# Two more tile pairs in the feed-forward blocks of a hybrid layer: FFN 2's tiles 2 and 3, and a fifth pair in FFN 1's w2

## The chip, the cores and the metric

The kernel runs on one core of one Trainium2 chip. The metric is the device time of one execution in microseconds, the median of several runs. A core has five engines with instruction queues of their own: TensorE (PE; its weight loads are shown as PEld), VectorE (DVE), ScalarE (ACT), GpSimd (POOL) and SyncE (SP), which here issues nearly all DMA transfers. Each queue is worked off in order, and engines wait for each other through semaphores.

## The reference

One layer on 512 tokens with a model width of 1024, all in float32:

```
f = swiglu(rms_norm(x, g1), w1a, w3a, w2a)        # FFN 1, hidden width 2816
h = x + 0.5 * rms_norm(f, post1)
u = rms_norm(h, mix_pre)
q, k, v, x_rnn, x_gate = split(u @ w_in)
y_a = (rg_lru(causal_conv(x_rnn)) * gelu(x_gate)) @ w_lru_out
y_b = sliding_window_attention(q, k, v, sinks, bias) @ w_attn_out
g = sigmoid(u @ w_gate + b_gate)
h = h + rms_norm((g[0] * y_a + g[1] * y_b) @ w_o, mix_post)
f = swiglu(rms_norm(h, g2), w1b, w3b, w2b)        # FFN 2, the same shape
y = h + 0.5 * rms_norm(f, post2)

swiglu(x, w1, w3, w2) = (silu(x @ w1) * (x @ w3)) @ w2
```

## The kernel before

Every float32 operand is split into a rounded part ("hi", in the fp32r format) and a remainder ("lo"): ScalarE rounds, VectorE subtracts. A product is then three matmuls: hi x hi, lo x hi, hi x lo. Activations lie transposed in one big buffer, uT (hi and lo, 8 blocks of 128 features, 512 tokens). Everything else lives in a pool of 43 equal buffers of 4 KB per partition (`NSLOT`), which are taken when a tile is first written and come free after its last reader.

The hidden width of 2816 is 22 tiles of 128. A tile of w1 or w3 is worked in one of two ways.

- A plain *unit* (`unit`, `mm_feat`): 8 blocks x 3 matmuls with 512 columns, 24 matmuls.
- A *pair job* (`class Pairs`): two neighbouring tiles of one matrix are multiplied with x as a 2 x 2 block product after Strassen and Winograd, with 7 products in place of 8. A product (`mm_s`) is 12 matmuls with 256 columns, so a job is 84 matmuls. For x it needs the blocks b11, b21, b22 and the sums t1 to t4 (`sums`, `to_slots`, `to_uT`). For the weights it needs sums and differences of the four blocks, split into hi and lo. `prep(m, i)` makes these for job m in five steps (0: four sums; 1 to 3: one tile split each; 4: half a tile), and `run` calls those of the next job between the products of the current one. The product with t4 of a job is issued behind the second product of the following job.

`NC1 = 6` and `NC2 = 4` say how many tiles of FFN 1 and FFN 2 go as plain units; the others are pair jobs (16 and 18 of them).

The last product of an FFN, hidden x w2 (`w2_gemm`), has four token tiles by two halves of 512 columns, accumulated in all eight PSUM banks. `W2` gives its order: so many plain tiles, then groups of tile pairs (again 7 products for 8; here a pair is 42 matmuls of 512 columns, where two plain tiles are 48), then plain tiles, then the last `RF` tiles, which `tok_finish` works token tile by token tile, so that norm and transposes of one token tile run beside the next one's matmuls. FFN 1 has 6 plain tiles, one group of 4 pairs, 2 plain tiles and 6 last ones. FFN 2 has 2, two groups of 4 pairs, and 4 last ones. A plan inside `w2_gemm` with costs and due times orders the splits, sums and differences for VectorE and ScalarE.

For some pairs of w2 the weight parts t1 and t2, b22, t3 and t4 are made long before, in stages with free time, stored to device memory and loaded again when needed (`pre_pair`, `PRE`, `PRE_AT`): FFN 2's pairs 2, 4, 6, 8 and 14.

Work that is to run beside the matmuls is put off with `later(n, fn, rank)`: it is emitted at the n-th `point()` from there. Points lie after half a unit (12 matmuls) or after one product of a pair job; among work due at one point the lower rank goes first.

`post_norm` takes the mean square of a token tile from PSUM (ScalarE squares and sums two halves), gets the reciprocal root through a square root, a reciprocal and one Newton step on VectorE, and adds the residual. `norms` does this and then the next block's first norm. Before FFN 2 the code runs the output projection `wo` by `tok_gemm`, whose end works the first two tiles of w1b and w3b in half-units of 256 columns.

Of the kernel before, what the change touches and what calls it, by code (L numbers as in the profile page):

```python
# [12 lines left out]
AF = mybir.ActivationFunctionType  # L13
ALU = mybir.AluOpType

P = 128
SEQ = 512
D = 1024
# [8 lines left out]
EPS = 1e-6  # L27
# [24 lines left out]
def hybrid_layer(ctx: ExitStack, tc: tile.TileContext, a: dict, out: bass.AP):  # L52
# [126 lines left out]
    def later(n, fn, rank=1):  # L179
        uid[0] += 1  # L180
        due.append((now[0] + n, rank, uid[0], fn))
# [63 lines left out]
    def bcast(name):  # L245
# [2 lines left out]
        pool.dma_start(out=t, in_=bass.AP(tensor=src.tensor, offset=src.offset, ap=[[0, P], [1, D]]))  # L248
        return t

    def post_norm(acc, res, gpost, scale, dst, after=None):

        ss = small(2, "ss")
        fg = slot([P, D], name="fg")
        junk = slot([P, D], name="junk")
        cs = [slice(n * 512, (n + 1) * 512) for n in range(2)]
        for n, c in enumerate(cs):
            act.activation(junk[:, c], acc[n], AF.Square, accum_out=ss[:, n : n + 1])
        dve.tensor_tensor(out=fg[:, cs[0]], in0=acc[0], in1=gpost[:, cs[0]], op=ALU.mult)
        s1 = small(1, "s1")  # L260
        dve.tensor_tensor(out=s1, in0=ss[:, 0:1], in1=ss[:, 1:2], op=ALU.add)
        r = rstd_of(s1, scale, lambda: dve.tensor_tensor(out=fg[:, cs[1]], in0=acc[1], in1=gpost[:, cs[1]], op=ALU.mult))
        for n in range(2):
            c = slice(n * 512, (n + 1) * 512)
            dve.scalar_tensor_tensor(out=dst[:, c], in0=fg[:, c], scalar=r, in1=res[:, c], op0=ALU.mult, op1=ALU.add)
            if after:
                after(n, c)

    def norms(acc, t, res, gpost, scale, gpre, keep):

        hg = slot([P, D], name="hg")
        junk = slot([P, D], name="junk")
        ss = small(2, "ss")

        def half(n, c):
            act.activation(junk[:, c], res[:, c], AF.Square, accum_out=ss[:, n : n + 1])
            dve.tensor_tensor(out=hg[:, c], in0=res[:, c], in1=gpre[:, c], op=ALU.mult)

        post_norm(acc, res, gpost, scale, res, half)
        sp.dma_start(out=keep[t], in_=res)  # L280
        s1 = small(1, "s1")
        dve.tensor_tensor(out=s1, in0=ss[:, 0:1], in1=ss[:, 1:2], op=ALU.add)
        r = rstd_of(s1)
        dve.tensor_scalar(out=hg[:, :512], in0=hg[:, :512], scalar1=r, scalar2=None, op0=ALU.mult)
        act.activation(hg[:, 512:], hg[:, 512:], AF.Copy, scale=r)
        return hg
# [147 lines left out]
    def pre_pair(nm, f, at0, step):  # L434
        made = PRE_TILES.setdefault(nm, {})
        dram = [tc.dram_tile([P, D], F32, name=f"pre_{nm}{f}_{i}") for i in range(5)]
        made[f] = [dram[:2], *dram[2:]]
        r, t = [], {}

        def load():  # L440
            for n in range(2):
                r.append(slot([P, D], name="rawp"))
                src = a[nm][f * P : (f + 2) * P, n * 512 : n * 512 + 512]
                sp.dma_start(out=r[n].rearrange("p (b c) -> p b c", b=2), in_=src.rearrange("(b p) c -> p b c", p=P))

        def hi(name, src, w=QH):
            if w == D:
                t[name] = slot([P, D], F32R, name="ph"), slot([P, D], F32R, name="pl")
            else:
                x = slot([P, 2, QH], F32R, name="pb")  # L450
                t[name] = x[:, 0, :], x[:, 1, :], x
            t[name] = *t[name], src
            act.activation(t[name][0], src, AF.Copy)

        def lo(name):
            x = t[name]
            dve.tensor_tensor(out=x[1], in0=x[-1], in1=f32(x[0]), op=ALU.subtract)
# [12 lines left out]

        steps = [
            (load,),
            (),
            (lambda: hi("t12", t12_of(*r), D),),
            (lambda: lo("t12"), lambda: hi("b22", r[1][:, QH:])),
            (lambda: store(0, "t12"), lambda: lo("b22")),
            (sums34, lambda: store(1, "b22")),
            (lambda: lo("t3"), lambda: hi("t4", r[0][:, QH:])),
            (lambda: store(2, "t3"), lambda: lo("t4"), lambda: r.clear()),
            (lambda: store(3, "t4"),),  # L480
        ]
        for i, fns in enumerate(steps):
            later(at0 + i * step, lambda fns=fns: [fn() for fn in fns], 4)

    def pre_at(where):
        for nm, f, at_, step in PRE_AT.get(where, ()):
            pre_pair(nm, f, at_, step)

# [347 lines left out]
    QH = 4 * P  # L836
# [13 lines left out]
    class Pairs:  # L850
# [13 lines left out]
        def prep(self, m, i):  # L864
            if m >= len(self.jobs):
                return
            k = self.k0 + 2 * m
            if i == 0:
# [119 lines left out]
    def load_w(u, kp):  # L988
        nm, i = order[u]
        c = slice(kp * 2 * P, (kp + 1) * 2 * P)  # L990
        sp.dma_start(out=raw3[u][:, c], in_=a[nm][i * P : (i + 1) * P, c])


    warm = slot([P, 512], F32R, name="warm")
# [3 lines left out]
        pe.matmul(psw, warm[:, :P], warm, start=True, stop=True)  # L998

    load_x(0, act)  # L1000
    sp.dma_start(out=vec, in_=a["vec"])
    for kp in range(KT // 2):
        load_w(0, kp)
        if kp:
            load_x(2 * kp)
        load_w(1, kp)
        load_w(2, kp)
        load_x(2 * kp + 1)
    dma_to(NS + 2)
# [4 lines left out]
    hid, X1 = Hidden("w2a"), {}  # L1014
# [115 lines left out]
    def uview(hh, th):  # L1130

        return lambda e, k: uT[:, e, 4 * hh + k, th * 256 : th * 256 + 256]
# [1 line left out]
    def pair_view(p):  # L1134
        return lambda e, k: p[e][:, k, :]

    def sums(xf):

        t = [slot([P, 4, 256], name="T") for _ in range(4)]
        dve.tensor_tensor(out=t[0], in0=xf[0, 1], in1=xf[0, 0], op=ALU.subtract)  # L1140
        dve.tensor_tensor(out=t[2], in0=xf[1, 1], in1=xf[0, 1], op=ALU.subtract)
# [43 lines left out]
    def w2_ahead():  # L1185
# [301 lines left out]
    def emit_step(n):  # L1487
# [2 lines left out]
            bias_load(g + 1)  # L1490
        att_s(g, j)

    w_lru = get("lru", 0)
    point(True)
    bias_load(0)
# [44 lines left out]
    hid = Hidden("w2b")  # L1540
    X2, tn = {"b11": uview(0, 0), "b21": uview(1, 0), "b22": uview(1, 1)}, []
# [3 lines left out]
    later(2, lambda: xf.clear())  # L1545
    for i in range(3):
        later(2 + i, lambda i=i: X2.update({f"t{i + 1}": to_slots(tn[i])}))
    pairs_b = Pairs("w1b", "w3b", NC2, X2, hid)
    end = 2 * 2 * (NC2 - 2)
    for i, at_ in enumerate((end - 7, end - 4, end - 3, end - 2, end - 1)):  # L1550
        later(at_, lambda i=i: pairs_b.prep(0, i))
    later(end, lambda: pairs_b.prep(1, 0))
    swiglu_units("w1b", "w3b", 2, NC2, hid)
    point(True)
    X2["t4"] = to_uT(tn[3], 0, 1)
    tn.clear()
    pairs_b.run(w2_ahead)
    X2 = pairs_b = None
    w2_gemm("w2b", hid, "ffn2_post_g", 0.5, None, [], h2, None)


# [16 lines left out]
W2_LOAD = (14, 9, 8, 8)  # L1578
P0A, P0B = 6, 8
W2_LEAD = 2.5  # L1580
# [1 line left out]
W2_FLUSH = 2.5  # L1582

NC1 = 6
NC2 = 4


# [52 lines left out]
```

## Time and profile before

| | |
|---|---|
| median of 3 runs | 1120.51 us (1120.48 to 1120.9) |
| the profiled execution | 1120.09 us, span 1118.3 us |
| granted TensorE clock, mean | 0.999 |
| TensorE busy / its weight loads busy | 99% / 88% of the span |
| VectorE / ScalarE / GpSimd busy | 81% / 54% / 3% |
| instructions on TensorE | 6613 matmuls, 6613 weight loads |

The span runs from the first to the last instruction; some 1.8 us of the execution lie around it. Matmuls are pipelined, and their ends are modelled: one that is shown with 0.39 us may start 0.23 us after the one before, so the spacing of the starts is what a matmul costs. The stages follow each other so: FFN 1's w1 and w3 to 234 us, its w2 to about 350 us, the mixer's projections, recurrent branch and attention to about 724 us, `wo` to 799 us, FFN 2's w1 and w3 to 1002 us, its w2 to the end.

### The profile page before, as it was taken

The numbers are of one execution on the slowest core, as the hardware profiler recorded it, in microseconds if no ns is written. First come the engines' busy times: TensorE is split into PE (matmuls) and PEld (weight loads), VectorE is DVE, ScalarE is ACT, GpSimd is POOL, SyncE is SP. The second block draws the span as 40 slices with busy tenths as digits, with TensorE's granted clock in tenths as the row PEclk, the third lists the DMA queues.
The fourth block names the chain that finished last, engine by engine and source line by source line (L and its number), as shares of the span: only waits on it lengthen the run. The fifth ranks groups of instructions, "written<-read, shape, count | busy, mean of one in ns | idle before, by whom it ended". The sixth has DMA issues, their size and how long they took to land.

```text
span 1118.3 us, 17215 instructions
## 1 busy us (share of the span) xinstructions
PE 1109.7 (99%) x6613; PEld 987.7 (88%) x6613; DVE 907.3 (81%) x1609; ACT 607.8 (54%) x1072; POOL 34.7 (3%) x60
## 2 busy tenths in 40 slices
PE   9999999999999999999999999999999999999997
PEld 7889999988889887888888888888999999998886
DVE  5999888888887777886799877777868888887995
ACT  7555555564455368945655664355644555555352
POOL 0000000000000000001021111000000000000000
PEclk9999999999999999999999999999999999999999
DMA  9863332260554444536232335562333322357543
GB/s 343 148 165 102 114 96 94 77 225 1 173 203 159 162 156 149 182 117 225 76 95 76 95 95 218 199 241 79 133 121 104 114 90 101 95 205 268 178 177 113
DMA packets 50482, 161.12 MB, mean 144 GB/s; under 512 B 5536, under 2 KB 7072, under 8 KB 50400
## 3 DMA queue, kind: packets, MB, share of 16 engines
q1 hardware_dynamic: 47808, 151.33, 39.3%
q0 software_dynamic: 2448, 8.43, 4.0%
q8 instruction: 52, 0.85, 0.3%
q10 hardware_dynamic: 144, 0.26, 0.1%
q14 instruction: 30, 0.25, 0.1%
HBM read 136.42 MB, written 22.54 MB: 142 GB/s over the span
## 4 chain that ended last, share of the span: by engine, by line
PE 98%; ACT 1%; DMA 1%; DVE 0%; DVEq 0%; issue 0%
PE f L205 12%; PE f L207 12%; PE f L206 12%; PE c L845 10%; PE c L847 10%; PE c L846 10%; PE acc L223 5%; PE acc L224 5%; PE acc L225 5%; PE acc L719 3%; PE acc L721 3%; PE acc L720 3%; PE pt L1446 1%; PE s L1410 1%; DMA t<-pre_w2b 1%; PE tr L294 1%
## 5 line engine op out<-in xcount | busy, mean ns | idle before, releaser
L205 PE MATMUL f<-uT,whi 128*128 128x512 f32 (+1 forms) x536 | 196.7, 367 | 0.0
L207 PE MATMUL f<-uT,whi 128*128 128x512 f32 (+1 forms) x536 | 195.2, 364 | 0.0
L206 PE MATMUL f<-uT,wlo 128*128 128x512 f32 (+1 forms) x536 | 195.1, 364 | 0.0
L205 PEld LDWEIGHTS f<-uT,whi 128*128 128x128 f32 x536 | 101.2, 189 | 16.9 <-issue 1.4
L845 PE MATMUL c<-Xh,whi 128*128 128x256 f32 x408 | 115.6, 283 | 0.1
L847 PE MATMUL c<-uT,whi 128*128 128x256 f32 x408 | 115.5, 283 | 0.0
L846 PE MATMUL c<-Xh,wlo 128*128 128x256 f32 x408 | 115.5, 283 | 0.0
L846 PE MATMUL c<-uT,wlo 128*128 128x256 f32 x408 | 115.5, 283 | 0.0
L847 PE MATMUL c<-Xl,whi 128*128 128x256 f32 x408 | 115.5, 283 | 0.0
L845 PE MATMUL c<-uT,whi 128*128 128x256 f32 x408 | 115.5, 283 | 0.0
L207 PEld LDWEIGHTS f<-uT,whi 128*128 128x128 f32 x536 | 101.1, 189 | 16.2
L206 PEld LDWEIGHTS f<-uT,wlo 128*128 128x128 f32 x536 | 101.2, 189 | 15.6
L196 DVE TENSOR_TENSOR wlo<-S,whi 128x1024 fp32r<-128x1024 f32 x68 | 82.9, 1219 | 16.4 <-ACT whi L195 16.4
L845 PEld LDWEIGHTS c<-Xh,whi 128*128 128x128 f32 x408 | 78.3, 192 | 0.3 <-ACT ct L920 0.3
L846 PEld LDWEIGHTS c<-uT,wlo 128*128 128x128 f32 x408 | 78.3, 192 | 0.0
L845 PEld LDWEIGHTS c<-uT,whi 128*128 128x128 f32 x408 | 78.3, 192 | 0.0
L846 PEld LDWEIGHTS c<-Xh,wlo 128*128 128x128 f32 x408 | 78.3, 192 | 0.0
L847 PEld LDWEIGHTS c<-uT,whi 128*128 128x128 f32 x408 | 78.3, 192 | 0.0
L847 PEld LDWEIGHTS c<-Xl,whi 128*128 128x128 f32 x408 | 78.3, 192 | 0.0
L195 ACT ACTIVATE whi<-S 128x1024 fp32r<-128x1024 f32 x68 | 68.2, 1050 | 0.0
L223 PE MATMUL acc<-whi,hT 128*128 128x512 f32 x160 | 62.5, 390 | 0.0
L224 PE MATMUL acc<-wlo,hT 128*128 128x512 f32 x160 | 62.3, 389 | 0.0
(406 smaller groups left out, 2741.6 us busy)
## 6 DMA issues: line engine op xcount, KB each, us to landing
raw_w2a<-in_w2a_dram SPq DMA_DIRECT2D x22, 512.0 KB, 4.6
raw_w1b<-in_w1b_dram SPq DMA_DIRECT2D x22, 512.0 KB, 4.5
raw_w3b<-in_w3b_dram SPq DMA_DIRECT2D x22, 512.0 KB, 4.5
raw_w3a<-in_w3a_dram SPq DMA_DIRECT2D x21, 512.0 KB, 4.2
raw_w1a<-in_w1a_dram SPq DMA_DIRECT2D x20, 512.0 KB, 4.6
raw_w2b<-in_w2b_dram SPq DMA_DIRECT2D x17, 512.0 KB, 4.1
h<-h SPq DMA_DIRECT2D x16, 512.0 KB, 3.7
raw_wg<-in_wg_dram SPq DMA_DIRECT2D x16, 512.0 KB, 3.9
```

Of the source, the lines that this page charges most:

```text
L195: act.activation(hi, src, AF.Copy)
L196: dve.tensor_tensor(out=lo, in0=src, in1=f32(hi), op=ALU.subtract)
L205: pe.matmul(ps[:, c0:c1], wh[:, s], h_, start=k == 0, stop=False)
L206: pe.matmul(ps[:, c0:c1], wl[:, s], h_, start=False, stop=False)
L207: pe.matmul(ps[:, c0:c1], wh[:, s], l_, start=False, stop=k == KT - 1)
L223: pe.matmul(acc[n], x[:, 0, c], wh[:, s], start=first, stop=False, skip_group_check=True)
L224: pe.matmul(acc[n], x[:, 0, c], wl[:, s], start=False, stop=False, skip_group_check=True)
L225: pe.matmul(acc[n], x[:, 1, c], wh[:, s], start=False, stop=last, skip_group_check=True)
L719: pe.matmul(b, h[:, c], wh, start=start and n_ == 0, stop=False, skip_group_check=True)
L845: pe.matmul(ps, wh[:, s], xh, start=first, stop=False, skip_group_check=True)
L846: pe.matmul(ps, wl[:, s], xh, start=False, stop=False, skip_group_check=True)
L847: pe.matmul(ps, wh[:, s], xl, start=False, stop=k == 3, skip_group_check=True)
```

## The change

- FFN 2's tiles 2 and 3 are no longer plain units but a pair (`NC2 = 2`, 20 pair jobs). The first job's weights are loaded and prepared during the attention output projection (`FIRST_AT`, with a new step -1 of `prep` that only loads). The sums of x are made directly behind `wo`, with t1 split in between, and t3 and t4 are split inside the first job.
- FFN 1's w2 has one group of 5 pairs in place of 4 and no plain tiles behind it. The first of the five (tile 6) has its parts made during FFN 1's pair jobs 9 to 15 in finer steps (`PRE_JOB`), stored, and loaded in w2.
- FFN 2's stored pairs 2, 8 and 14 are made in the x_rnn stage from points 1, 6 and 11 on; pair 14 was made in the attention output stage, pairs 2 and 8 from points 2 and 8 on.
- The norms get a shorter chain: the first half's mean square is scaled as soon as it is there, ScalarE's square root takes it as bias, constant factors move into the scaling of the data, and the Newton step is one instruction shorter.
- At the start one of the first weight blocks is issued from ScalarE's queue instead of SyncE's.

The core of the diff:

```diff
+    def sum_half(ss, n, junk, src, c):
+        act.activation(junk[:, c], src, AF.Square, accum_out=ss[:, n : n + 1])
+    def first_half(ss):
+        v0 = small(1, "v0")
+        dve.tensor_scalar(out=v0, in0=ss[:, 0:1], scalar1=1.0 / D, scalar2=EPS, op0=ALU.mult, op1=ALU.add)
+        return v0
+    def root(ss, v0):
+        s = small(1, "s")
+        act.activation(s, ss[:, 1:2], AF.Sqrt, scale=1.0 / D, bias=v0)
+        return s
+    def factor(ss, v0, s):
+        v, r, e, r2 = (small(1, x) for x in ("v", "r", "e", "r2"))
+        dve.scalar_tensor_tensor(out=v, in0=ss[:, 1:2], scalar=1.0 / D, in1=v0, op0=ALU.mult, op1=ALU.add)
+        dve.reciprocal(r, s)
+        dve.scalar_tensor_tensor(out=e, in0=r, scalar=v, in1=r, op0=ALU.mult, op1=ALU.mult)
+        dve.scalar_tensor_tensor(out=r2, in0=e, scalar=-3.0, in1=r, op0=ALU.add, op1=ALU.mult)
+        return r2
...
     def post_norm(acc, res, gpost, scale, dst, after=None):
...
+        for n in range(2):
+            sum_half(ss, n, junk, acc[n], cs[n])
+        scaled(0)
+        v0 = first_half(ss)
+        s = root(ss, v0)
+        scaled(1)
+        r = factor(ss, v0, s)
...
+        if nm == "w2a":
+            s = []
+            steps = [
+                (load,), (), (),
+                (lambda: s.append(slot([P, D], name="T12")), sub(lambda: s[0][:, :QH], lambda: r[1][:, :QH], lambda: r[0][:, :QH])),
+                (sub(lambda: s[0][:, QH:], lambda: r[1][:, QH:], lambda: s[0][:, :QH]),),
+                (lambda: hi("t12", s.pop(), D),),
+                (lambda: lo("t12"),),
+                (lambda: store(0, "t12"), lambda: hi("b22", r[1][:, QH:])),
+                (lambda: lo("b22"),),
+                (lambda: store(1, "b22"), sub(lambda: r[1][:, :QH], lambda: r[1][:, QH:], lambda: r[1][:, :QH])),
+                (lambda: hi("t3", r[1][:, :QH]), sub(lambda: r[0][:, QH:], lambda: r[0][:, QH:], lambda: r[0][:, :QH])),
+                (sub(lambda: r[0][:, QH:], lambda: r[0][:, QH:], lambda: r[1][:, :QH]),),
+                (lambda: hi("t4", r[0][:, QH:]), lambda: lo("t3")),
+                (lambda: store(2, "t3"), lambda: lo("t4"), lambda: r.clear()),
+                (lambda: store(3, "t4"),),
+            ]
...
     def pre_at(where):
+        for i, at_ in FIRST_AT.get(where, ()):
+            later(at_, lambda i=i: pairs_b.prep(0, i), 5)
...
     load_x(0, act)
+    load_w(1, 0, act)
...
+    pre_at("w1a")
     pairs_a.run(w2_ahead, late)
...
-    later(1, lambda: hid.f.append(silu_mul(bs[0], bs[1])))
-    later(2, lambda: hid.f.append(silu_mul(bs[2], bs[3])))
-    later(1, lambda: tn.extend(sums(xf)))
...
-    swiglu_units("w1b", "w3b", 2, NC2, hid)
...
-    pairs_b.run(w2_ahead)
+    tn.extend(sums(xf, X2))
+    xf.clear()
+    hid.f.append(silu_mul(bs[0], bs[1]))
+    X2["t2"] = to_slots(tn[1])
+    pairs_b.prep(1, 0)
+    hid.f.append(silu_mul(bs[2], bs[3]))
+    late = {
+        (0, 2): [lambda: X2.update(t3=to_slots(tn[2]))],
+        (0, 3): [lambda: X2.update(t4=to_uT(tn[3], 0, 1)), tn.clear],
+    }
+    pairs_b.run(w2_ahead, late)
...
+FIRST_AT = {"wao": ((-1, 0), (0, 3), (1, 5), (2, 7), (3, 9), (4, 10))}
-W2 = {"w2a": (6, (4,), 6, 0.95), "w2b": (2, (4, 4), 4, 0.95)}
+W2 = {"w2a": (6, (5,), 6, 0.95), "w2b": (2, (4, 4), 4, 0.95)}
-PRE = {"w2b": (2, 4, 6, 8, 14)}
-PRE_AT = {"xr": [("w2b", 2, 2, 2), ("w2b", 8, 8, 2)], "xg": [("w2b", 4, 7, 1)], ("wg", 13): [("w2b", 6, 1, 1)], "wao": [("w2b", 14, 4, 1)]}
+PRE = {"w2a": (6,), "w2b": (2, 4, 6, 8, 14)}
+PRE_JOB = (0, 1, 2, 9, 11, 19, 21, 26, 28, 29, 33, 34, 40, 42, 43)
+PRE_AT = {"w1a": [("w2a", 6, 63, PRE_JOB)], "xr": [("w2b", 2, 1, 2), ("w2b", 8, 6, 2), ("w2b", 14, 11, 2)], "xg": [("w2b", 4, 7, 1)], ("wg", 13): [("w2b", 6, 1, 1)]}
-NC2 = 4
+NC2 = 2
```

More of the change, by code (lines that the diff above doesn't have):

```diff
@@ L256, in post_norm, with scaled @@
         cs = [slice(n * 512, (n + 1) * 512) for n in range(2)]
-        for n, c in enumerate(cs):
[L258 to L264, printed above, removed]
+        def scaled(n):
+            dve.scalar_tensor_tensor(out=fg[:, cs[n]], in0=acc[n], scalar=-0.5 * scale, in1=gpost[:, cs[n]], op0=ALU.mult, op1=ALU.mult)
+        for n in range(2):
[5 more added lines that the diff above has]
+        r = factor(ss, v0, s)
+        for n, c in enumerate(cs):
             dve.scalar_tensor_tensor(out=dst[:, c], in0=fg[:, c], scalar=r, in1=res[:, c], op0=ALU.mult, op1=ALU.add)
@@ L273, in norms @@
         ss = small(2, "ss")
+        v0 = []
         def half(n, c):
-            act.activation(junk[:, c], res[:, c], AF.Square, accum_out=ss[:, n : n + 1])
-            dve.tensor_tensor(out=hg[:, c], in0=res[:, c], in1=gpre[:, c], op=ALU.mult)
+            sum_half(ss, n, junk, res[:, c], c)
+            if n:
+                v0.append(first_half(ss))
+            dve.scalar_tensor_tensor(out=hg[:, c], in0=res[:, c], scalar=-0.5, in1=gpre[:, c], op0=ALU.mult, op1=ALU.mult)
         post_norm(acc, res, gpost, scale, res, half)
+        s = root(ss, v0[0])
         sp.dma_start(out=keep[t], in_=res)
-        s1 = small(1, "s1")
-        dve.tensor_tensor(out=s1, in0=ss[:, 0:1], in1=ss[:, 1:2], op=ALU.add)
-        r = rstd_of(s1)
+        r = factor(ss, v0[0], s)
         dve.tensor_scalar(out=hg[:, :512], in0=hg[:, :512], scalar1=r, scalar2=None, op0=ALU.mult)
@@ L481, in pre_pair, with sub @@
         ]
+        def sub(o, x, y):
+            return lambda: dve.tensor_tensor(out=o(), in0=x(), in1=y(), op=ALU.subtract)
+        if nm == "w2a":
[15 more added lines that the diff above has]
+            ]
         for i, fns in enumerate(steps):
-            later(at0 + i * step, lambda fns=fns: [fn() for fn in fns], 4)
+            later(at0 + (i * step if isinstance(step, int) else step[i]), lambda fns=fns: [fn() for fn in fns], 4)
     def pre_at(where):
+        for i, at_ in FIRST_AT.get(where, ()):
+            later(at_, lambda i=i: pairs_b.prep(0, i), 5)
         for nm, f, at_, step in PRE_AT.get(where, ()):
@@ L867, in prep @@
             k = self.k0 + 2 * m
+            if i < 0:
+                dma_one(k)
+                dma_one(k + 1)
+                return
             if i == 0:
@@ L986, in load_x, with load_w @@
         q.dma_start(out=xts[k // 2][:, k % 2, :], in_=a["xT"][k * P : (k + 1) * P, :])
-    def load_w(u, kp):
+    def load_w(u, kp, q=sp):
         nm, i = order[u]
         c = slice(kp * 2 * P, (kp + 1) * 2 * P)
-        sp.dma_start(out=raw3[u][:, c], in_=a[nm][i * P : (i + 1) * P, c])
+        q.dma_start(out=raw3[u][:, c], in_=a[nm][i * P : (i + 1) * P, c])
     warm = slot([P, 512], F32R, name="warm")
@@ L1005, in hybrid_layer @@
             load_x(2 * kp)
-        load_w(1, kp)
+            load_w(1, kp)
         load_w(2, kp)
@@ L1135, in pair_view, with sums @@
         return lambda e, k: p[e][:, k, :]
-    def sums(xf):
+    def sums(xf, X=None):
         t = [slot([P, 4, 256], name="T") for _ in range(4)]
         dve.tensor_tensor(out=t[0], in0=xf[0, 1], in1=xf[0, 0], op=ALU.subtract)
+        if X is not None:
+            X["t1"] = to_slots(t[0])
         dve.tensor_tensor(out=t[2], in0=xf[1, 1], in1=xf[0, 1], op=ALU.subtract)
@@ L1491, in emit_step @@
         att_s(g, j)
+    hid = Hidden("w2b")
+    X2, tn = {"b11": uview(0, 0), "b21": uview(1, 0), "b22": uview(1, 1)}, []
+    pairs_b = Pairs("w1b", "w3b", NC2, X2, hid)
     w_lru = get("lru", 0)
@@ L1537, in hybrid_layer @@
     bs = tok_gemm("wo", mg, KT, RO, "mix_post_g", 1.0, "ffn2_pre_g", [("w1b", 0), ("w3b", 0), ("w1b", 1), ("w3b", 1)], h1, h2, xf=xf)
-    hid = Hidden("w2b")
-    X2, tn = {"b11": uview(0, 0), "b21": uview(1, 0), "b22": uview(1, 1)}, []
-    later(1, lambda: hid.f.append(silu_mul(bs[0], bs[1])))
-    later(2, lambda: hid.f.append(silu_mul(bs[2], bs[3])))
-    later(1, lambda: tn.extend(sums(xf)))
[L1545 to L1552, printed above, removed]
-    swiglu_units("w1b", "w3b", 2, NC2, hid)
-    point(True)
-    X2["t4"] = to_uT(tn[3], 0, 1)
-    tn.clear()
-    pairs_b.run(w2_ahead)
-    X2 = pairs_b = None
+    tn.extend(sums(xf, X2))
[9 more added lines that the diff above has]
+    pairs_b.run(w2_ahead, late)
+    X2 = pairs_b = late = None
     w2_gemm("w2b", hid, "ffn2_post_g", 0.5, None, [], h2, None)
```

## The prediction

> **What bounds the kernel now.** First the page: busy times and the chain that ended last.
>
> ```profile
> PE 1109.7 (99%) x6613; PEld 987.7 (88%) x6613; DVE 907.3 (81%) x1609; ACT 607.8 (54%) x1072; POOL 34.7 (3%) x60
> ...
> PE 98%; ACT 1%; DMA 1%; DVE 0%; DVEq 0%; issue 0%
> ```
>
> TensorE is on the chain for 98% of 1118.3 us. A busy share can hide small gaps, so next the waits, those of the weight loads:
>
> ```profile
> PEld tr L294 <- DVE hg L284: 0.6, 2, 0.3
> PEld acc L719 <- DMA t<-pre_w2b: 0.5, 1, 0.5
> PEld f L1046 <- ACT uT L1039: 0.4, 1, 0.4
> ...
> PEld c L845 <- ACT ct L920: 0.3, 1, 0.3
> ```
>
> Nothing that TensorE waits for comes to a microsecond. Time is therefore lost or won in two ways: by fewer matmuls, or by a helper engine (VectorE above all) coming late. The third view is a table by stretch, which prices a matmul and shows how full VectorE is:
>
> ```profile
> core 0: us, PE busy (x) PEld busy (x) DVE busy (x) ACT busy (x) POOL busy (x), PEclk, DMA share, GB/s
> 798.69:820.47 21.78, 21.78 (x98) 18.02 (x97) 15.20 (x19) 7.32 (x9) 0.00 (x0) 1.00 0.28 102
> 820.47:1001.91 181.44, 181.44 (x1514) 181.43 (x1513) 148.16 (x218) 94.50 (x156) 0.00 (x0) 1.00 0.33 106
> 266.69:304.78 38.09, 38.09 (x169) 31.53 (x168) 30.50 (x49) 17.99 (x30) 1.10 (x2) 1.00 0.36 112
> 304.78:315.66 10.88, 10.88 (x49) 9.01 (x48) 10.88 (x14) 9.06 (x12) 0.00 (x0) 1.00 1.01 363
> 236.20:315.70 79.50, 79.50 (x353) 65.80 (x352) 69.71 (x106) 39.59 (x60) 1.10 (x2) 1.00 0.41 141
> 100.00:200.00 100.00, 100.00 (x836) 100.00 (x835) 85.70 (x142) 51.59 (x85) 0.00 (x0) 1.00 0.32 102
> 425.00:450.00 25.00, 25.00 (x120) 19.70 (x119) 19.40 (x31) 21.42 (x31) 0.00 (x0) 1.00 0.46 148
> ```
>
> By the code the first stretch is FFN 2's tiles 2 and 3 as four plain units (96 matmuls of 512 columns; the counts take in a neighbour at each edge): 21.78 us, 227 ns a matmul. The second is its 18 pair jobs, 84 matmuls of 256 columns each: 181.44 / 18 = 10.08 us a job, 120 ns a matmul. The third is FFN 1's group of four tile pairs in w2, 168 matmuls: 9.52 us a pair. The fourth is the two plain tiles behind it, 48 matmuls: 10.88 us. The granted clock is 1.00 in all.
>
> **The change, part by part.** *FFN 2's tiles 2 and 3.* Four units (21.78) become two pair jobs (2 x 10.08 = 20.16): 1.62 us less, if the weights and inputs are there.
>
> *FFN 1's w2.* Two plain tiles (10.88) become a fifth pair (9.52): 1.36 us less. Both together: 2.98 us.
>
> A 256-column matmul takes 120 ns where half of a 512-column one would be 113.5. In the pair jobs weight loads fill 181.43 of 181.44 us, in the units 18.02 of 21.78. The Trainium skill (Perfetto Trace Analysis, Matmuls) says that larger matmuls are more efficient than smaller ones; that speaks against this change, and the rows bear it out: at 113.5 ns a job would be 9.53 us and the two jobs would save 2.72. The Trainium skill (TensorE: Matmul & The Clock Gate, Back-to-back issue gap) gives N/2.4 + 2.5 ns between warm matmuls. By that a job is 84 x 109.2 ns = 9.17, two units 48 x 215.8 = 10.36, so an estimate of 2.4 us for two jobs and 1.3 for w2, 3.7 in all; the trace has 120 and 227, and I stay with it.
>
> *The fifth pair's parts, made in FFN 1's pair jobs.* Before's own stored pairs give the price of the five differences, three half-width remainders and the full-width one:
>
> ```profile
> L457 DVE TENSOR_TENSOR pb<-rawp,pb x15: 678/684/1232, 401.5 to 719.3; 128x512 fp32r<-128x512 f32 x15
> L423 DVE TENSOR_TENSOR T<-rawp,rawp x5: 681/685/692, 389.1 to 698.5; 128x512 f32<-128x512 f32 x5
> ```
> ```profile
> L457 DVE TENSOR_TENSOR pl<-T,ph x5: 1214/1220/1226, 397.0 to 706.0; 128x1024 fp32r<-128x1024 f32 x5
> ```
>
> 5 x 0.69 + 3 x 0.68 + 1.22 = 6.7 us of VectorE. Between 100 and 200 us it is busy 85.70 of 100, so 1.44 us of each 10.08 us job is free. The new steps lie on 43 points, one per product of 12 matmuls (1.44 us): 62 us, some six jobs, 8.8 us free. The densest job (points 28 to 34) gets a remainder and three differences, 2.7 us, and runs 1.3 us late. Its cover is the lead of the weights; here one remainder and the matmul that uses it:
>
> ```profile
> 167.90 1.23 DVE L196 TENSOR_TENSOR wlo<-raw_w1a,whi 128x1024 fp32r<-128x1024 f32 x1 [0.88 <-ACT whi L195]
> ```
> ```profile
> 172.22 0.28 PE L846 MATMUL c<-Xh,wlo 128*128 128x256 f32 x1
> ```
>
> 172.22 - 169.13 = 3.1 us, more than 1.3. ScalarE's roundings of these parts come 2 to 8 points behind the differences they read, so it does not block the copies of PSUM that follow. Cost 0; were the lead gone, 1.3. SyncE gets two loads and five stores more; with the DMA share at 0.32 I count 0.
>
> *FFN 1's w2 stage.* VectorE is busy 69.71 of 79.50 us, 9.8 idle. At the prices above the fifth pair adds at most 1.22 + 8 x 0.69 = 6.7 and the two plain tiles take away 2 x (0.68 + 1.22) = 3.8; the stage is 1.4 shorter. Idle left: 5.5. Cost 0; the case against is rival 2.
>
> *FFN 2's opening.* The four units were the cover under which its inputs and first weights were made. Now job 0's weights are made in the attention output, where the stored pair 14 was made until now (7.1 us of VectorE for 6.7, so no change), and its two loads go out at that stage's first point. Pair 14's 6.7 us move to points 11 to 27 of the x_rnn stage, two points to a 5.45 us unit: 44 us, VectorE from 19.40 to some 23.2 of 25 us there. It ranks behind that point's other work; at worst one 1.22 us remainder is ahead of what TensorE wants; taken as 0.
>
> What still lies between the last transposes and job 0, in order, starts here:
>
> ```profile
> 785.37 2.48 DVE L304 TENSOR_TENSOR uT<-tr,uT 128x512 fp32r<-128x512 f32 x4 [0.75 <-ACT uT L303]
> ...
> 794.13 1.21 DVE L1140 TENSOR_TENSOR T<-xf,xf 128x1024 f32<-128x1024 f32 x1
> ```
>
> VectorE is free at 787.9, the copies it needs are there about 0.4 later. Then t1's difference, ScalarE's rounding and the remainder (1.2 + 1.1 + 1.2), three differences (3.6), 795.4; a SiLU product (0.7), t2's remainder (1.2), 797.3; job 1's sums (2.8) and a product (0.7), 800.8. Job 0 would start at 798.69 and needs t1 at 800.13, t2 at 801.57, t3 (remainder done near 804.5) at 805.9. Job 1 starts at 807.3 and needs its first weights (done near 805.7) then and the second (near 808.1) at 808.8, with t4's remainder between the two. The tightest place has 0.7 us. FFN 1's opening, which does the same, cost the 0.3 us wait of L845 shown above. I take 0.2, between 0 and 0.8.
>
> *The norms.* Only the last one has no matmul beside it. After: mean square, root and square share a step less (the sum and one scaling go). What decides is when VectorE may read the second half:
>
> ```profile
> 756.34 0.69 DVE L259 TENSOR_TENSOR fg<-acc,bc_mix_post_g 128x512 f32<-128x512 f32 x1 [0.90 <-ACT junk L258]
> ...
> 1112.36 0.68 DVE L262 TENSOR_TENSOR fg<-acc,bc_ffn_post_g 128x512 f32<-128x512 f32 x1
> 1112.95 0.15 DVE L235 RECIPROCAL r<-s 128x1 f32<-128x1 f32 x1
> ...
> 1113.78 1.42 DVE L265 SCALAR_TENSOR_TENSOR o<-fg,r,h 128x512 f32<-128x512 f32 x2
> ```
> ```profile
> 1111.87 0.19 ACT L258 ACTIVATION_READ_ACCUMULATOR junk<-acc 128x1 f32 x1
> ```
>
> At 756.34 VectorE waits for ScalarE's square of the same bank. So the scaling of the second half starts at about 1112.1 where it starts at 1112.36; behind it come four small steps at some 0.2 where there were four from 1112.95 on, one of them new. Gain 0.15; if the read need not wait it starts near 1111.4, gain at most 0.5; at least 0. In the other norms a shorter chain takes away at most the 0.6 us of waits on hg, which are prefetches of weights: 0. The first weight block that goes from SyncE's queue to ScalarE's touches the 0.4 us wait of L1046, which waits for another load: 0 to -0.1, taken as 0.
>
> The sum, against the profiled execution (1120.09 us: 1118.3 of span and 1.8 around it): -1.62 - 1.36 - 0.15 + 0.2 = -2.93, so 1117.2. The median of the runs is 0.42 above that execution; from it 1120.51 - 2.93 = 1117.6. No change is anything within 0.2%, 2.24 us.
>
> **The rivals.** *1: FFN 2's opening comes late, and the gain is eaten.* In before, one raw tile of this stage waits for a buffer:
>
> ```profile
> 784.50 11.82 SPq L142 DMA_DIRECT2D raw_w3b<-in_w3b_dram  x2
> ```
> ```profile
> raw_w3b<-in_w3b_dram SPq DMA_DIRECT2D x22, 512.0 KB, 4.5
> ```
>
> Its second issue is near 796.3 and lands 4.5 later, 800.8. Were that job 1's tile, its sums would start 3.5 us later than in my list (797.3), with everything behind them; against the 0.7 us that are spare, TensorE waits 2.8, that is 2.6 more than forecast: 1120.2, no change. Against it: the splits of the four units, which held buffers then, are gone. For it: job 0's seven made tiles hold buffers now.
>
> *2: FFN 1's group of five runs out of buffers, and the change is slower.* Counted by hand from the code, when the last pair's t1 and t2 are made, products b11 and b21 of five pairs (10 tiles), t1 and t2 of five (10), raw tiles of four pairs (8), hidden tiles (8), their parts (5) and the kept copies and differences (4) want 45 of 43 buffers. The engines are in order, so VectorE stops until b11 and b21 are let go.
>
> ```profile
> 270.41 1.23 DVE L505 TENSOR_TENSOR bl<-T,bh 128x1024 fp32r<-128x1024 f32 x1 [0.52 <-ACT bh L508]
> ...
> 302.26 0.70 DVE L678 TENSOR_TENSOR acc<-acc,kp 128x512 f32<-128x512 f32 x1 [1.39 <-PE acc L721]
> ```
>
> In before the last of these is done at 271.6; one more pair puts it near 276. The group starts at 266.69, its first two products take 2 x 6.8 us: the first buffers come free near 277.6, the last at 280.3. From there 41 half-width steps (12 additions, 17 remainders, 12 differences; at the 0.69 above 28.3 us, less where they overlap) and six tiles (6 x 1.9) lie ahead, which I put at 37 us with that overlap, as against the last tile's first use at 317.9: in time by some 2 us from 277.6 (with 1 us for ScalarE's rounding first), but late by 0.7 from 280.3, and by 4.9 with three waits for products like the 1.39 above. A second stop as long as the first (280.3 - 277.6 = 2.7), until t1 and t2 are let go, makes it 7.6: 1117.4 (the forecast without its 0.2) + 7.6 = 1125.0. It decides from 5.4 us of waiting on (3.1 + 2.24).
>
> **How the numbers follow.** The forecast, 0.64: faster. Rival 1, 0.20: no change. Rival 2, 0.16: slower. So faster by over 0.2% 0.64, within 0.2% 0.20, slower 0.16. The forecast's own range is 1116.9 (tail 0.5, start 0.1, no wait) to 1118.2 (opening 0.8). The range leaves out rival 2 and little else: 1116.7 to 1120.7.
>
> **What would show it.** Right: 6613 matmuls become 6679 (96 and 6 of 512 columns go, 168 of 256 come); FFN 2's first product starts straight behind the last half-units; the group of five runs 210 matmuls in 47.6 us without a gap and the last phase follows at once; the second half's scaling at the end starts within 0.2 us of the square's end. Wrong: waits of the weight loads on ScalarE or VectorE in FFN 2's first two jobs (rival 1), or in w2's group and the phase behind it, near 300 to 318, with VectorE idle near 276 to 280 (rival 2). A saving near 3.7 us would say that the pair jobs' matmuls are cheaper than 120 ns.

## The result and the profile after

| | before | after |
|---|---|---|
| median of 17 runs | 1120.48 us (1120.09 to 1121.13) | 1118.57 us (1118.26 to 1118.9) |
| the profiled execution | 1120.09 us, span 1118.3 | 1118.27 us, span 1116.5 |
| matmuls | 6613 | 6679 |

The ratio is 0.9982, with a 95% interval of 0.9976 to 0.9989: 1.91 us less, where 2.93 were forecast. By the prediction's own bound (0.2%, 2.24 us) that is no change; the time is 1.0 us above the forecast and inside its range.

The page of the changed kernel, busy times and chain:

```profile
PE 1107.2 (99%) x6679; PEld 988.6 (89%) x6679; DVE 920.1 (82%) x1622; ACT 617.2 (55%) x1088; POOL 34.7 (3%) x60
...
PE 94%; ACT 3%; DVE 2%; issue 1%; DMA 0%; DVEq 0%; SPq 0%; ACTq 0%
```

TensorE's share of the chain falls from 98% to 94%: the chain now makes a detour over ScalarE and VectorE. Where it does so stands in the waits of the weight loads. The kernel before had at r only single waits of 0.4 us, and none at V:

```profile
PEld r L1304 <- ACT ig_e L1308: 1.3, 2, 0.9
...
PEld v L1407 <- DVE wlo L161: 1.0, 1, 1.0
```

r are the products of the recurrent block's gates, v those of V. Both lie in the stretch from 425 to 475 us, to which pair 14 was moved. The table by stretch of the changed kernel (columns as in the prediction) has FFN 1's group of five, FFN 2's 20 pair jobs, and that stretch in two halves:

```profile
266.69:314.29 47.60, 47.60 (x212) 39.41 (x210) 41.02 (x62) 23.75 (x37) 1.10 (x2) 1.00 0.44 146
799.06:1000.67 201.61, 201.61 (x1683) 201.61 (x1682) 166.64 (x246) 106.52 (x175) 0.00 (x0) 1.00 0.32 105
425.00:450.00 25.00, 24.51 (x116) 18.87 (x115) 20.55 (x33) 22.31 (x33) 0.00 (x0) 1.00 0.42 147
450.00:475.00 25.00, 24.22 (x151) 21.78 (x151) 19.98 (x30) 24.62 (x39) 0.00 (x0) 1.00 0.57 177
```

The group runs its 210 matmuls in 47.60 us and the jobs take 201.61 / 20 = 10.08 us each, all at a granted clock of 1.00 and without a gap. In the last two rows TensorE isn't busy throughout. VectorE has over 4 us free in each of them. The matmuls at the three gaps there:

```profile
447.85 0.39 PE L1304 MATMUL i<-xcs,rghi 64*128 64x512 f32 x1
448.73 0.47 PE L1304 MATMUL r<-xcs,rghi 64*128 64x512 f32 x1 [0.49 <-DVE xcs L1295]
...
449.37 0.49 PE L1304 MATMUL i<-xcs,rghi 64*128 64x512 f32 x1
449.79 0.50 PE L205 MATMUL f<-uT,whi 128*128 128x512 f32 x1
...
459.55 0.28 PE L1406 MATMUL v<-whi,uT 128*128 128x256 f32 x1
460.62 0.39 PE L1407 MATMUL v<-wlo,uT 128*128 128x256 f32 x1 [0.78 <-DVE wlo L161]
```

From start to start that is 0.88 and 0.42 us where 0.23 is usual, and 1.07 where 0.12 is: 0.65, 0.19 and 0.95 lost, 1.8 us in all. The matmuls right behind each gap also come a little wider apart: from a product ahead of the three gaps (400.17 us before, 398.91 after) to one behind them (530.06 and 530.80) the changed kernel loses 2.0 us.

Now the engines behind it, in order of time. ScalarE of the changed kernel:

```profile
438.27 0.82 ACT L1324 ACTIVATE xc_t<-xc_t,chalf 128x512 f32<-128x512 f32 x1
441.26 0.63 ACT L484 ACTIVATE pb<-rawp 128x512 fp32r<-128x512 f32 x1 [2.17 <-DVE rawp L459]
441.80 0.67 ACT L1308 ACTIVATE xc_t<-r,bhalf 64x512 f32<-64x512 f32 x1
...
443.92 0.68 ACT L1308 ACTIVATE ig_e<-i,bhalf 64x512 f32<-64x512 f32 x1
...
450.54 0.62 ACT L484 ACTIVATE pb<-rawp 128x512 fp32r<-128x512 f32 x1
```

VectorE of the changed kernel:

```profile
439.94 0.69 DVE L1296 TENSOR_TENSOR xcs<-xc_t,xcs 128x512 fp32r<-128x512 f32 x1
440.55 0.68 DVE L459 TENSOR_TENSOR rawp<-rawp 128x512 f32<-128x512 f32 x1
...
444.63 0.69 DVE L1309 SCALAR_TENSOR_TENSOR ig_e<-ig_e,xc_t 128x512 f32<-128x512 f32 x1 [2.08 <-ACT ig_e L1308]
...
448.16 0.42 DVE L1295 CAST xcs<-xc_t 128x512 fp32r<-128x512 f32 x1
...
456.95 0.69 DVE L1309 SCALAR_TENSOR_TENSOR ig_e<-ig_e,xc_t 128x512 f32<-128x512 f32 x1 [2.85 <-ACT ig_e L1308]
...
459.35 1.22 DVE L161 TENSOR_TENSOR wlo<-raw_wv,whi 128x1024 fp32r<-128x1024 f32 x1
```

L484 is a pre-made pair's rounding of t3, L459 the first of the differences that it needs. Both are issued at the same point (`sums34`). ScalarE reaches the rounding at 439.09 and stands for 2.17 us, since VectorE, itself in order, has other work until 440.55. The four gate functions (L1308) are behind it in ScalarE's queue and, once it is done, start without a wait of their own; VectorE needs the gates for its step L1309, and behind that step are the copy xcs (L1295) for which TensorE waits at r, and the weights' remainders. Before had no rounding there, and its gates (then L1246) followed the same function (then L1262) at once:

```profile
439.58 0.82 ACT L1262 ACTIVATE xc_t<-xc_t,chalf 128x512 f32<-128x512 f32 x1
440.30 0.67 ACT L1246 ACTIVATE xc_t<-r,bhalf 64x512 f32<-64x512 f32 x1
```

That is 0.72 us from start to start before, and 441.80 - 438.27 = 3.53 after: the gates are 2.81 us late. VectorE's own standing is nothing new. Before, it stood even longer at the same step (then L1247):

```profile
443.13 0.69 DVE L1247 SCALAR_TENSOR_TENSOR ig_e<-ig_e,xc_t 128x512 f32<-128x512 f32 x1 [2.35 <-DMA raw_wq<-in_wq_dram]
```

The profile names a load as the last to be waited for, but the last gate, which the step reads, had ended only at 443.10. So ScalarE sets the pace of this step in both kernels, and from the function's start (L1262, L1324) to the step's start it is 3.55 us before and 6.36 after: the same 2.81 more. At V the delay is carried on. ScalarE has no wait from 441.26 to 457 us in which to catch up, it has one more rounding in that time (450.54), and VectorE, after standing 2.85 us for the next gates (2.93 before), comes late to the remainder at 459.35.

A page of the Trainium skill (Perfetto Trace Analysis, Per-instruction lifecycle) says that a slice holds the execution and not the wait for semaphores ahead of it. The trace agrees: the rounding that stood for 2.17 us is shown with 0.63.

### The profile page after: what moved, and what is told of

Its sections match the earlier page's. It is cut to its first block, busy times and chain, and to the rows that moved or that the text cites. A ratio compares the mean times of both kernels' runs of the same rounds, so it can differ in the third digit from the quotient of the medians.

```text
span 1116.5 us, 17407 instructions
## 1 busy us (share of the span) xinstructions
PE 1107.2 (99%) x6679; PEld 988.6 (89%) x6679; DVE 920.1 (82%) x1622; ACT 617.2 (55%) x1088; POOL 34.7 (3%) x60
## 4 chain that ended last, share of the span: by engine, by line
PE 94%; ACT 3%; DVE 2%; issue 1%; DMA 0%; DVEq 0%; SPq 0%; ACTq 0%
PE c L899 11%; PE c L901 11%; PE c L900 11%; PE f L205 10%; PE f L206 10%; PE f L207 10%; PE acc L223 4%; PE acc L225 4%; PE acc L224 4%; PE acc L774 4%; PE acc L773 4%; PE acc L775 4%; PE pt L1508 1%; ACT ig_e L1308 1%; PE s L1472 1%; PE s L1471 1%
## 5 line engine op out<-in xcount | busy, mean ns | idle before, releaser
L205 PE MATMUL f<-uT,whi 128*128 128x512 f32 (+1 forms) x504 | 184.3, 366 | 0.0
L207 PE MATMUL f<-uT,whi 128*128 128x512 f32 (+1 forms) x504 | 182.7, 362 | 0.0
L206 PE MATMUL f<-uT,wlo 128*128 128x512 f32 (+1 forms) x504 | 182.7, 362 | 0.0
L899 PE MATMUL c<-Xh,whi 128*128 128x256 f32 x432 | 122.4, 283 | 0.1
L899 PE MATMUL c<-uT,whi 128*128 128x256 f32 x432 | 122.4, 283 | 0.0
L901 PE MATMUL c<-Xl,whi 128*128 128x256 f32 x432 | 122.3, 283 | 0.0
L900 PE MATMUL c<-Xh,wlo 128*128 128x256 f32 x432 | 122.3, 283 | 0.0
L901 PE MATMUL c<-uT,whi 128*128 128x256 f32 x432 | 122.3, 283 | 0.0
L900 PE MATMUL c<-uT,wlo 128*128 128x256 f32 x432 | 122.3, 283 | 0.0
L205 PEld LDWEIGHTS f<-uT,whi 128*128 128x128 f32 x504 | 95.1, 189 | 15.7 <-issue 1.3
L207 PEld LDWEIGHTS f<-uT,whi 128*128 128x128 f32 x504 | 95.1, 189 | 15.0
L899 PEld LDWEIGHTS c<-uT,whi 128*128 128x128 f32 x432 | 83.0, 192 | 0.0
L901 PEld LDWEIGHTS c<-uT,whi 128*128 128x128 f32 x432 | 83.0, 192 | 0.0
L223 PE MATMUL acc<-whi,hT 128*128 128x512 f32 x144 | 56.2, 390 | 0.0
```

The source lines that it names most:

```text
L205: pe.matmul(ps[:, c0:c1], wh[:, s], h_, start=k == 0, stop=False)
L206: pe.matmul(ps[:, c0:c1], wl[:, s], h_, start=False, stop=False)
L207: pe.matmul(ps[:, c0:c1], wh[:, s], l_, start=False, stop=k == KT - 1)
L223: pe.matmul(acc[n], x[:, 0, c], wh[:, s], start=first, stop=False, skip_group_check=True)
L899: pe.matmul(ps, wh[:, s], xh, start=first, stop=False, skip_group_check=True)
L900: pe.matmul(ps, wl[:, s], xh, start=False, stop=False, skip_group_check=True)
```

## The experiments

Three theories on where the missing 1.0 us went. A: the moved pair 14, by ScalarE's standing. B: the x_rnn stage goes at ScalarE's own pace and gives back whatever TensorE gains ahead of it (it arrives earlier now, thanks to FFN 1). C: FFN 2's opening or FFN 1's group gives less than it should. In theory A it was open whether the waiting counts or the added work.

**Pair 14's move alone (x_alone).** The kernel before with the new points of the x_rnn stage, which also puts pairs 2 and 8 one and two points earlier:

```diff
-PRE_AT = {"xr": [("w2b", 2, 2, 2), ("w2b", 8, 8, 2)], ..., "wao": [("w2b", 14, 4, 1)]}
+PRE_AT = {"xr": [("w2b", 2, 1, 2), ("w2b", 8, 6, 2), ("w2b", 14, 11, 2)], ...}
```

> The kernel before with one edit: FFN 2's pre-made pair 14 is made in the x_rnn stage (pairs 2, 8 and 14 at points 1, 6 and 11) instead of in the attention projection's stage. Theory A (the moved pair holds ScalarE up in order: its rounding waits there for VectorE's difference, the gates behind it come late, and TensorE waits in the x_rnn to V stage for 0.65 + 0.19 + 0.95 us): slower by about 1.8 us, 1122.3 us, with TensorE waits at the r products and at V. Theory B (that stage goes at ScalarE's own pace and gives back whatever TensorE gained ahead of it; TensorE came there some 1.9 us earlier in the changed kernel): TensorE isn't early here, so no change, 1120.3 to 1120.7 us. Theory C (the shortfall lies in FFN 2's opening or in FFN 1's group of five): no change here either.

1122.43 us against 1120.59; ratio 1.0017 (1.0008 to 1.0026): 1.84 us slower. Its profile, ScalarE and then TensorE's waits:

```profile
442.94 0.63 ACT L453 ACTIVATE pb<-rawp 128x512 fp32r<-128x512 f32 x1 [2.17 <-DVE rawp L428]
```
```profile
PE v L1345 <- DVE wlo L161: 0.8, 1, 0.8
PE r L1242 <- DVE xcs L1233: 0.5, 1, 0.5
```

The same standing and the same waits, in a kernel in which TensorE isn't early: A, and neither B nor C.

**Everything but FFN 2's part (no_ffn2).** The kernel before with FFN 1's fifth pair, the new norms and the start's new queue; pair 14 and `NC2` as before.

> The changed kernel without FFN 2's part: FFN 1's fifth pair, the new norms and the start's new queue on the kernel before, pair 14 where it was before. Theory A: no wait in the x_rnn stage, so the sum of the three parts alone: -1.36 (pair), -0.37 (tail's norm), -0.2 (start) = 1118.6 us. Theory B: TensorE comes to the x_rnn stage 1.6 us earlier than in the kernel before and waits there for most of it: 1119.7 to 1120.2 us. Theory C in the form that FFN 1's group of five gives less than its 1.36: 1119 to 1120 us without waits in the x_rnn stage.

1118.42 us against 1120.59; ratio 0.9981 (0.9973 to 0.999): -2.17. TensorE comes early to the x_rnn stage and doesn't wait there: in its profile the same matmul starts 1.09 us earlier than in the kernel before at 400 us, and still 1.09 earlier at 530 us. B falls.

**Pair 14 back in its old place (a_back).** The changed kernel with

```diff
-"xr": [("w2b", 2, 1, 2), ("w2b", 8, 6, 2), ("w2b", 14, 11, 2)]
+"xr": [("w2b", 2, 2, 2), ("w2b", 8, 8, 2)], "wao": [("w2b", 14, 4, 1)]
```

> The changed kernel with pairs 2 and 8 at the points they had and pair 14 back in the attention projection's stage, beside the new preparation of FFN 2's first row products. Theory A: the 1.8 us of waits in the x_rnn to V stage are gone, 1116.8 us, unless the projection's stage, which now holds both, waits for buffers (then 1117 to 1119, with waits of TensorE or an idle VectorE at some 790 to 830 us). Theory B: the waits in the x_rnn stage stay, since TensorE comes as early as in the changed kernel: 1118.3 to 1118.8 us. Theory C: 1118.6 us.

1121.09 us against 1120.59; ratio 1.0004 (0.9995 to 1.0013): slower than any of the theories had it. The x_rnn stage is free of waits again, but the attention output stage now has some, from 721 us on and so earlier than expected. The waits of the weight loads, and ScalarE:

```profile
PEld acc L223 <- DVE g L1587: 1.6, 1, 1.6
...
PEld f L206 <- DVE wlo L161: 1.4, 1, 1.4
PEld acc L224 <- DVE wlo L161: 0.9, 2, 0.8
PEld f L205 <- ACT whi L160: 0.8, 1, 0.8
```
```profile
718.56 0.63 ACT L484 ACTIVATE pb<-rawp 128x512 fp32r<-128x512 f32 x1 [1.42 <-DVE rawp L459]
...
721.09 1.04 ACT L160 ACTIVATE whi<-raw_wao 128x1024 fp32r<-128x1024 f32 x1
```

Between 721 and 738 us the matmuls' starts have gaps of 3.7 us in all. Once more the rounding of t3 stands for its difference; behind it are three more roundings, two of them for FFN 2's first job, and then that of the weight block (whi) for which TensorE waits. So the change couldn't have left pair 14 there as it was. How much of the 3.7 us is this standing and how much the double load of VectorE and ScalarE wasn't told apart.

**The rounding of t3 apart from its difference (a_split).** The changed kernel, for pair 14 alone, with in effect

```diff
-            (sums34, lambda: store(1, "b22")),           # differences, then the rounding of t3
+            (lambda: t34_of(*r), lambda: store(1, "b22")),
+            (lambda: hi("t3", r[1][:, :QH]),),           # two points later, as all that follows
```

> The changed kernel with one edit: pair 14's differences for t3 and t4 are issued one point after the step before, and the rounding of t3 one point (2 places) later than its difference, so that ScalarE no longer stands behind VectorE for it; the work is the same. Theory A in its first form (the 2.17 us in which ScalarE stood for the difference are what delays the gates): most of the waits go, 1116.8 to 1117.4 us. Theory A in its second form (it is the two more roundings of 0.63 us each on a ScalarE that has no idle time from 441 to 462 us): 1118.0 to 1118.6 us, waits as before. Theory B: 1118.6 us.

1116.79 us against 1120.59; ratio 0.9966 (0.9952 to 0.9979): 1.78 less than the changed kernel. ScalarE, and VectorE's differences:

```profile
438.80 0.82 ACT L1333 ACTIVATE xc_t<-xc_t,chalf 128x512 f32<-128x512 f32 x1
439.52 0.67 ACT L1317 ACTIVATE xc_t<-r,bhalf 64x512 f32<-64x512 f32 x1
...
448.27 0.61 ACT L484 ACTIVATE pb<-rawp 128x512 fp32r<-128x512 f32 x1
...
451.87 0.61 ACT L484 ACTIVATE pb<-rawp 128x512 fp32r<-128x512 f32 x1
```
```profile
441.05 0.68 DVE L459 TENSOR_TENSOR rawp<-rawp 128x512 f32<-128x512 f32 x1
```

The gates start 0.72 us after the function ahead of them, as in the kernel before. Two roundings of pre-made pairs lie between 441 and 462 us as in the changed kernel (there at 441.26 and 450.54), on a ScalarE that is as full (20.28 us busy in these 21 us there, 20.56 here); only now neither waits. So the added work as such costs no time that shows. The edit takes away the standing and also puts the rounding itself behind the gates; but of the 2.81 us by which the gates were late, the rounding is only 0.54 (441.26 to 441.80) and the standing 2.17.

**The move with the rounding apart, on the kernel before (x_split).** x_alone and the edit of a_split.

> The kernel before with pair 14 made in the x_rnn stage, as in the run with that alone (1122.43 us, +1.84), and here with t3's rounding a point (two places) after its difference. Theory A in its first form (ScalarE, in order, stands for VectorE's difference, and the gates stand behind it): nothing is lost, 1120.4 to 1120.9 us. In its second form (the added work itself): 1121.8 to 1122.5 us.

1120.2 us against 1120.49; ratio 0.9997 (0.9988 to 1.0006). No cost of the move can be told when the rounding doesn't stand: 1.84 us with, none without. On the changed kernel the same edit is worth 1.78.

**The parts alone.** FFN 1's fifth pair (p_ffn1: `W2`, `PRE`, `PRE_JOB` and the finer steps on the kernel before):

> The kernel before with FFN 1's part alone: the group of five pairs, the fifth pair's parts made within the pair jobs, the old norms and the old start. By the prediction's term -1.36 us, 1119.2 us, if the term is sized right. If the group of five gives less (a late part, a buffer), 1119.5 to 1120.6 with waits of TensorE in w2's group; if some of what the three parts without FFN 2 gave together (-2.17 us for FFN 1's pair, norms and start) is really the pair's, 1118.4 to 1118.9.

1119.18 us against 1120.49; ratio 0.9988 (0.9979 to 0.9996): -1.31, with -1.36 expected.

The norms (p_norms: `post_norm` and `norms` of the changed kernel in the kernel before):

> The kernel before with the new norms alone. The prediction took -0.15 us (0 to -0.5) for the tail and 0 elsewhere: 1120.4 us. The profile of the changed kernel has 2.04 us from the last square's start to the first output's start, where before had 2.41: -0.37, 1120.2 us. If the norms also help or hurt at the transposes between stages, further from it than that.

1119.81 us against 1120.49; ratio 0.9994 (0.9985 to 1.0003). -0.68 in the medians, not told apart from -0.37 or from nothing. In its profile the tail takes 2.04 us as in the changed kernel.

The start (p_start: `load_w(1, 0, act)` alone):

> The kernel before with one weight block of the start on ScalarE's queue, ahead of the others. The prediction took 0 to -0.1 us. In the profile of the changed kernel the first product after the warming ones starts 0.1 us earlier and the first waits are shorter: -0.1 to -0.3 us, 1120.3 to 1120.5 us, within what can be told from no change.

1120.12 us against 1120.49; ratio 0.9999 (0.999 to 1.0007): no difference can be told.

**All roundings apart (a_split_all), beside the changed kernel on the same chip (after_again).** For pairs 2, 8 and 14 the rounding of t1 and t2 also gets a point of its own:

```diff
-            (lambda: hi("t12", t12_of(*r), D),),
+            (lambda: s.append(t12_of(*r)),),
+            (lambda: hi("t12", s.pop(), D),),
```

> The changed kernel with a rounding a point after its differences for every one of the three pairs made in the x_rnn stage (2, 8 and 14), at t1/t2 and at t3, where the run with this for pair 14's t3 alone gave 1116.79 us. There ScalarE still stood 4.8 us for VectorE's differences of t1 and t2 in this stage, without a wait of TensorE. If standing costs only where the gates are due behind it (theory A as it now is): no gain more, 1116.4 to 1117.1 us, ScalarE's standing gone. If standing of ScalarE costs by itself: up to 1 us less, below 1116.2. If the later points push pair 14's parts onto other work of the stage: 1117.3 to 1118.5 with new waits.

> The changed kernel itself, on the same chip as the version with all roundings apart, so that the two stand side by side: 1118.6 us, as in its own runs, with the waits at the r products and at V in its profile (0.65 + 0.19 + 0.95 us). Were the 1.8 us that the rounding's place is worth only a difference between chips, the two would come out within 0.4 us of each other here.

1116.28 us (ratio 0.9961, 0.9949 to 0.9974) and 1118.75 us (0.9981, 0.9972 to 0.999), against 1120.58: 2.5 us between the two on one chip. Between 400 and 480 us ScalarE stood 4.8 + 4.6 us for differences of these pairs in the changed kernel, and not at all here:

```profile
ACT ph L484 <- DVE T L455: 4.8, 2, 3.8
ACT pb L484 <- DVE rawp L459: 4.6, 3, 2.2
```

Yet all but 0.5 us of the gain came with the 2.17 us of pair 14's t3; a_split still had the first of these two lines, and 2.4 us of the second. The intervals of the two versions overlap, so whether the 0.5 is real stays open. As these runs show it, standing costs where something due is behind it. Both versions are faster than the kernel before and the changed one.

## Why the prediction was right and wrong

*Right: the two terms that make the gain.* FFN 2's tiles as a pair: no_ffn2 to a_split (both without loss in the x_rnn stage) is 1118.42 - 1116.79 = 1.63, forecast 1.62. FFN 1's fifth pair: 1.31, forecast 1.36. The medians aren't that exact, and so close an agreement is in part luck. The stretches of the profiles carry it without that noise: FFN 2's tiles from 2 on took 21.78 + 181.44 = 203.22 us before and 201.61 after, 1.61 less; FFN 1's group took 38.09 + 10.88 = 48.97 and 47.60, 1.37 less. By the Trainium skill's spacing (TensorE: Matmul & The Clock Gate, Back-to-back issue gap) it would have been an estimate of 3.7, which the runs refute: the jobs took 120 ns a matmul after as before. The page gives that formula for a matmul by itself and says that in a stream of weight loads and matmuls both set the spacing; here every matmul has its weight load (6679 of each), so the prediction used the formula outside its case.

*Wrong: one step.* It is the sentence on pair 14's move: "It ranks behind that point's other work; at worst one 1.22 us remainder is ahead of what TensorE wants; taken as 0." It measured 1.84 us (x_alone). The step weighed VectorE's load, 23.2 of 25 us forecast, and only asked what VectorE would do late. Ranking behind the work of its own point does not help against work of the next point: the rounding was behind everything due at its point and still ahead of the gates due at the next. VectorE's load, that the step did weigh, was no problem (20.55 of 25 us). For FFN 1's fifth pair the prediction did ask the question ("ScalarE's roundings of these parts come 2 to 8 points behind the differences they read"), and there nothing stood; for the moved pair, whose old steps issue both at one point, it didn't.

*Mis-sized: the tail's norm.* 0.15 forecast, 0.37 in the trace. The rows of the changed kernel:

```profile
1110.09 0.60 ACT L253 ACTIVATE junk<-acc 128x512 f32<-128x512 f32 x1 [2.03 <-PE acc L225]
...
1110.81 0.69 DVE L284 SCALAR_TENSOR_TENSOR fg<-acc,bc_ffn_post_g 128x512 f32<-128x512 f32 x1 [1.97 <-ACT junk L253]
1111.42 0.15 DVE L270 SCALAR_TENSOR_TENSOR v<-ss,v 128x1 f32<-128x1 f32 x1
1111.49 0.15 DVE L271 RECIPROCAL r<-s 128x1 f32<-128x1 f32 x1
...
1112.13 1.41 DVE L294 SCALAR_TENSOR_TENSOR o<-fg,r,h 128x512 f32<-128x512 f32 x2
```

The square in the kernel before:

```profile
1111.37 0.60 ACT L258 ACTIVATE junk<-acc 128x512 f32<-128x512 f32 x1 [2.03 <-PE acc L225]
```

From the square's start to the output's start it is 2.04 us; before it was 1113.78 - 1111.37 = 2.41. The start of the scaling came as forecast (at the square's end: 0.72 after its start, before 0.99), which is 0.27. The other 0.10 is in the small steps; one of them was thought to cost its share, but v and the reciprocal don't depend on each other and start 0.07 us apart, not 0.2.

*Mis-sized: FFN 2's opening.* 0.2 forecast, nothing measured. TensorE's and VectorE's rows:

```profile
798.94 0.28 PE L207 MATMUL f<-uT,whi 128*128 128x256 f32 x1
799.06 0.28 PE L899 MATMUL c<-uT,whi 128*128 128x256 f32 x1
```
```profile
796.09 1.22 DVE L196 TENSOR_TENSOR Xl<-T,Xh 128x1024 fp32r<-128x1024 f32 x1
797.22 0.68 DVE L946 TENSOR_TENSOR S<-raw_w3b 128x512 f32<-128x512 f32 x1
...
799.88 0.68 DVE L852 TENSOR_TENSOR sw<-f,sw 128x512 f32<-128x512 f32 x1
```

The first product stands straight behind the last half-unit. t2's remainder ends at 797.31 (797.3 in the list of the prediction), and the last product at 800.56 (800.8).

*The rivals.* The first (a raw tile of the opening comes late) is refuted by the row at 797.22, which starts without idle time. The second (the group of five runs out of buffers) by the group's 47.60 us without a gap. The result fell to "no change" by a third way that none of the rivals named. That the time lies inside the stated range is therefore in part luck: the forecast's own range ended at 1118.2, and the stated one went on to 1120.7 for a late opening, which didn't come.

*A reading.* "Nothing that TensorE waits for comes to a microsecond" overlooks one row of the waits in the kernel before, 1.5 us for the tile of its first, warming matmuls (L998). It is 1.5 in all profiles and changes nothing here.

*The sum.* The forecast's -2.93 with these terms mended (-0.2 for the opening, -0.22 for the tail, +1.84 for pair 14) is -1.51; measured were -1.91. The runs of the norms (-0.68 in the medians) and of the start (-0.37) can't settle the 0.40 between them. The two profiles, whose spans differ by 1.8 us, say where their difference arises. The table goes by the starts of the same matmul in both, the one that ends each stretch:

| stretch | start of the matmul at its end, before and after (us) | change in it |
|---|---|---|
| up to FFN 1's group | 266.01, 266.01 | 0 |
| FFN 1's group of pairs, before with two plain tiles | 315.66, 314.29 | -1.37 |
| FFN 1's norm, up to the x_rnn stage | 400.17, 398.91 | +0.11 |
| x_rnn stage, V and a little on | 530.06, 530.80 | +2.00 |
| attention, `wo` | 745.03, 745.77 | 0 |
| norms behind `wo` | 789.09, 789.46 | -0.37 |
| FFN 2's pair jobs | 1002.14, 1000.89 | -1.62 |
| FFN 2's w2 | 1108.00, 1106.72 | -0.03 |
| the tail, from square to output | 2.41, 2.04 long | -0.37 |
| the output to the span's end | 4.52, 4.37 long | -0.15 |

So the new queue at the start gave nothing in this pair of profiles. The 0.37 behind `wo`, where the prediction had 0 for the norms, is only partly theirs: against the same profile of the kernel before, the four other profiles with the old norms also gain 0.20 to 0.28 there, and the seven with the new ones 0.30 to 0.38. That leaves about 0.1 us for the new norms. The rest is how this one execution of the kernel before went.

## What to carry to other kernels

On engines that work in order, moved work is not paid for when it fits into free time: ask of each instruction what it waits for and what is due behind it on its own engine. A producer and its consumer on two engines, issued together, make the second engine stand for the first one's whole queue; a point between them cost nothing here and was worth 1.8 us, nearly as much as the whole change. Look for such standing in the waits of the engine that isn't the bottleneck, and there only for those with due work behind them.

## What the runs showed of the hardware

A shorter stage can shift the next one's loads. In the seven profiles with FFN 1's group of five, the loads of xr's weights are issued from 307.2 to 307.6 us on, and the first block is rounded at 316.4 to 318.1 us. In the five without it the loads start at 304.9 to 306.1 us, and the rounding at 313.5 to 314.7. ScalarE in the kernel before, and in the changed kernel's second profile:

```profile
313.55 1.06 ACT L160 ACTIVATE whi<-raw_xr 128x1024 fp32r<-128x1024 f32 x1 [1.67 <-DMA raw_xr<-in_xr_dram]
```
```profile
318.09 1.06 ACT L160 ACTIVATE whi<-raw_xr 128x1024 fp32r<-128x1024 f32 x1 [5.12 <-DMA raw_xr<-in_xr_dram]
```
```profile
PEld tr L325 <- DVE hg L315: 1.0, 1, 1.0
```

The transposes of FFN 1's norm waited 1.0 us in this execution and 0.5 in the first one of the same kernel. That the late rounding is the cause isn't shown: they waited 0.8 us in a_split with a rounding at 316.45, and 0.3 in a_split_all with one at 317.31. And a load from device memory wasn't as steady as the engines: FFN 2's w2 waited for parts of stored pairs for 1.7 us (in two waits) in p_start's profile, 1.3 in that of p_ffn1 and 0.5 in that of before, and not at all in that of the changed kernel.

```profile
PEld acc L740 <- DMA t<-pre_w2b: 1.3, 1, 1.3
```
